# One place per half chunk instead of two for the output projection's matmuls in an RWKV-7 recurrence

## The chip, the cores and the metric

The kernel runs on one core of one Trainium2 chip. The metric is the device time of one execution in microseconds. Three runs of the kernel before gave 1660.01, 1664.27 and 1664.91 us, the median is 1664.27 us. One further execution was profiled; the rows below come from it.

## The reference, cut to what matters

One residual layer with an RWKV-7 mixer on 2048 tokens of width 1024, 16 heads of 64, in float32. The part around the change is the recurrence over tokens, the group norm of its output, the gate and the output projection:

```python
def step(S, inp):
    r_t, w_t, k_t, v_t, kk_t, a_t = inp
    sa = jnp.einsum('bhvk,bhk->bhv', S, -kk_t)
    S = (S * w_t[:, :, None, :]
         + sa[..., None] * (kk_t * a_t)[:, :, None, :]
         + v_t[..., None] * k_t[:, :, None, :])
    y_t = jnp.einsum('bhvk,bhk->bhv', S, r_t)
    return S, y_t
...
y = (y - mean) * lax.rsqrt(var + RW_GN_EPS)
y = y * gn_w.astype(f32).reshape(H, N) + gn_b.astype(f32).reshape(H, N)
y = y + jnp.sum(r_h * k_h * r_k.astype(f32), axis=-1, keepdims=True) * v_h
y = y.reshape(Bsz, T, W).astype(h.dtype) * g
return y @ w_out, v_first
...
x = x + y.astype(x.dtype)
```

## The kernel before

The tokens are cut into 64 chunks of 32. Earlier phases compute the projections and, for each chunk, small matrices that turn the recurrence within a chunk into matrix products; they go through memory and come back chunk by chunk (`load_c`, `load_v`, two and three chunks ahead). Chunks 0 to 8 run interleaved with the preparation of the last block of tokens. Chunks 9 to 63 run in the last phase, which is the one that the change touches. Its order on TensorE, VectorE, ScalarE and GpSimd is the order in which the program issues the instructions, and each engine works its queue in that order.

A chunk is done in two halves of 8 heads each (w = 0 and 1). Each half issues four small groups of 8 matmuls. A matmul of these groups is listed as two instructions in the trace, so a group is x16 there and x8 in the order:

- S, `r_state` (L249): the chunk's matrices times the state `x`, into `ybank`. Two ScalarE copies (L254) bring a part of it to `misc`.
- D, `r_d` (L274): the state's update, into `dp`. Two VectorE instructions (L51, x<-dp,misc) scale it into the next chunk's `x`. The D that stands behind S of one half belongs to the other half: behind S of w = 0 comes D of the chunk before, w = 1.
- Y, `r_y` (L289): the rest of the output, added to `ybank` of the other half. ScalarE copies it to `y` (L297).
- U, `r_u` (L261): a triangular product of `misc` into `ubank`. ScalarE copies it to `x` (L265), where the D and Y of the next half need it.

So U of a half waits for ScalarE's copies of S of the same half, D and Y wait for the copies of U of the half before, and S waits for VectorE's scaling of the D of the half before.

Every four chunks make a tile of 128 tokens, and `tail` turns it into background work: squares on ScalarE, sums on VectorE, a reciprocal root by Newton steps on GpSimd (L383, L384), normalisation and gating on VectorE, transposes on TensorE (L424), and in the end 48 projection matmuls (L460, 512 columns each: 2 output halves, 8 input blocks, 3 products of high and low parts), which go into the queue `dense`. `background` takes items of `work` for about 1.6 us of estimated time at each call, evacuations of finished output halves (L48) first. `fill(n)` takes n matmuls from `dense`, times 0.7, 1 or 1.3 by the queue's length, and keeps the rest as credit. Both are called by `chunk` through `state()`, which stands behind each S, and through `fill(i)`, which is the function `after` here: i = 0 behind D and i = 1 behind U in the first half, i = 2 and 3 in the second. After chunk 63 the program empties what is left.

`F` and `BG` are set as (2, 4) and 1.6.

Of the kernel before, what the change touches and what calls it, by code (L numbers as in the profile page):

```python
# [28 lines left out]
F, BG, EV, EV0, GWE, BNE, LOW, SLOW, FAST, INV, INVC = (2, 4), 1.6, (0, 0, 0), (0, 0, 0), 0, 0, 36, 0.7, 1.3, (8, 10), 0.5  # L29
# [10 lines left out]
def rwkv7_kernel(ctx, tc, a, T):  # L40
# [226 lines left out]
    def r_d(ch, w):  # L267
        if ch + 1 == NCH:
            return
        d, x = dk[ch % len(dk)], xs[ch % len(xs)]  # L270
        dp = bank[3]
        for p in range(4):
            for h in range(2):
                nc.tensor.matmul(dp[half(1 - h), p], d[:, h, 4 * w + p], x[:, h, 4 * w + p], start=True, stop=True,  # L274
                                 tile_position=(0, 64 * (1 - h)))
        g, c = divmod(ch, NC)
        with urgent():
            for h in range(2):

                H = half(1 - h)  # L280
                tt(xs[(ch + 1) % len(xs)][H, h, 4 * w : 4 * w + 4], dp[H],
                   pls[g][H, c, 4 * w : 4 * w + 4, None].broadcast_to([64, 4, N]), mul)

    def r_y(ch, w):
        st, x, c = stat[ch % len(stat)], xs[ch % len(xs)], ch % 4
        for p in range(4):
            for h in range(2):
                rb = bu(h)
                nc.tensor.matmul(bank[w][rb, ch % 2, p], st[rb, h, 4 * w + p, cr], x[rb, h, 4 * w + p], start=False,  # L289
                                 stop=(p == 3), skip_group_check=True, tile_position=(rb.start, rb.start))  # L290
        t = ch // 4
        if c == 0 and w == 0:
            new_y(t)
        with urgent():
            for h in range(2):
                o = 64 * h + L * (c % 2)
                ev(2, h)(ys[t][o : o + L, c // 2, 4 * w : 4 * w + 4], bank[w][bu(h), ch % 2])  # L297

    def chunk(ch, state, fill):

        g, c = divmod(ch, NC)
        if c == 2 and g + 1 < NB:
            load_g(g + 1)
        r_state(ch, 0)
        state()
        if ch != first[0]:
            r_d(ch - 1, 1)
        fill(0)
        if ch != first[0]:
            r_y(ch - 1, 1)  # L310
        if ch + 2 < NCH:
            load_v(ch + 2)
        if ch + 3 < NCH:
            load_c(ch + 3)
        r_u(ch, 0)
        fill(1)
        r_state(ch, 1)
        state()
        r_d(ch, 0)
        fill(2)  # L320
        r_y(ch, 0)
        r_u(ch, 1)
        fill(3)
# [4 lines left out]
    def fill(n):  # L328

        served[0] = min(served[0], 6) + n * (FAST if len(dense) > 2 * LOW else 1 if len(dense) > LOW else SLOW)  # L330
        while served[0] > 0 and dense:
            dense.popleft()[0]()
            served[0] -= 1
# [152 lines left out]
    def inversion(g, z, tmp):  # L486

        def load():
            for h in range(2):
                nc.sync.dma_start(z[half(h)], sm_d[g][bu(h), h, :, :, ca].rearrange("s c p t -> (c p) s t"))  # L490

        def step(j):
            n = L - 1 - j
            t3 = tmp()[:, 0 : j * n].rearrange("p (s t) -> p s t", t=n)
            tt(t3, z[:, 0:j, j : j + 1].broadcast_to([P, j, n]), z[:, j : j + 1, j + 1 :].broadcast_to([P, j, n]), mul)
            tt(z[:, 0:j, j + 1 :], z[:, 0:j, j + 1 :], t3, add)
            if j == 1:
                nc.vector.memset(z.rearrange("p s t -> p (s t)")[:, 0 : L * L : L + 1], 1.0)
                for h in range(2):
                    nc.sync.dma_start(sm_d[g][bu(h), h, :, :, ca].rearrange("s c p t -> (c p) s t"), z[half(h)])  # L500

        return [load] + [lambda j=j: step(j) for j in range(L - 2, 0, -1)]

    with ExitStack() as p0:
# [150 lines left out]
        with ExitStack() as pb:  # L655
            def pool(n, bufs, **k):
                return pb.enter_context(tc.tile_pool(name=n, bufs=bufs, reuse_waits="tile", **k))
# [380 lines left out]
            with tc.manual_schedule(engines=MANUAL):  # L1038
# [92 lines left out]
                def wo_split(p, q):  # L1131
                    hi, lo = (wo_t[x][p][:, 512 * q : 512 * q + 512] for x in range(2))
                    split(hi, lo, lo.bitcast(F32))
# [39 lines left out]
    with ExitStack() as p1:  # L1173
        def pool(n, bufs, **k):
            return p1.enter_context(tc.tile_pool(name=n, bufs=bufs, reuse_waits="tile", **k))

        c1, yp = pool("c1", 1), pool("yp", 1)
        sps, tps = pool("sps", 1, space=PSUM), pool("tps", 1, space=PSUM)
        for w in range(2):
            bank[w] = sps.tile([P, 2, 4, N], F32, name=f"ybank{w}")  # L1180
        bank[2] = sps.tile([P, 4, N], F32, name="ubank")
        bank[3] = sps.tile([P, 4, N], F32, name="dp")
        work = deque()
        evs[:] = EV
        al.update(rs=nc.gpsimd, newton=0, wait=2)
        al["sml"] = lambda nm: yp.tile([P, 2, NP], F32, name=nm, tag="sml", bufs=8)
        al["sq"] = lambda nm: yp.tile([P, 4, N], F32, name=nm, tag="big", bufs=4)
        al["v"] = lambda nm: yp.tile([P, NP, N], F32, name=nm, tag="v", bufs=4)
        al["o"] = lambda nm: yp.tile([P, NCT, P], F32R, name=nm, tag=nm[:2], bufs=2)
        al["yt"] = lambda nm: tps.tile([P, 4, P], F32, name=nm, tag="tps")  # L1190
        al["gt"] = lambda nm: yp.tile([P, NCT, 64], F32, name=nm, tag="gt", bufs=2)

        def background(us):

            served[1] = min(served[1] + us, us)
            fresh = True
            while evacs or work:
                u, fn = (evacs or work)[0]
                if not fresh and (u is None or u > served[1]):
                    break  # L1200
                (evacs or work).popleft()
                if u is None:
                    continue
                fresh = False
                fn()
                served[1] -= u

        def more_y(t):
            while t > 5 and t - 3 not in turned:
                background(1)  # L1210
            return yp.tile([P, 2, NP, N], F32, name=f"y{t}", tag="y", bufs=3)

        more[0], first[0] = more_y, NC + 1

        with tc.manual_schedule(engines=MANUAL):
            work.extend((0.7, lambda q=q: wo_split(NP - 1, q)) for q in range(2))
            for x in tail(1):
                work.extend(x)
            z = c1.tile([P, L, L], F32, name="z_")
            tm = c1.tile([P, 4 * N], F32, name="tm_")  # L1220
            inv = deque()
            for g in (NB - 2, NB - 1):
                load, *cols = inversion(g, z, lambda: tm)
                inv.extend([(0, load)] + [(None, None), (0, lambda: None)] * 4)
                inv.extend((INVC, x) for x in cols)
            inv_g = inv[L + 6][1]

            inv_last = inv[-1][1]

            def after(i):  # L1230
                if i % 2:
                    background(BG)
                fill(F[i % 2])

            for ch in range(NC + 1, NCH):
                chunk(ch, lambda: background(BG), after)
                if ch % 4 == 0 and ch > NC:
                    for x in tail(ch // 4 - 1):
                        work.extend(x)
                    for i in range(INV[1] if ch >= INV[0] else 0):  # L1240
                        if inv:
                            work.append(inv.popleft())
                if ch == NCH - 2 * NC - 4:
                    assert len(inv) <= L - 1 and not any(x[1] is inv_g for x in work)
                if ch == NCH - NC - 4:
                    assert not inv and not any(x[1] is inv_last for x in work)
            r_d(NCH - 1, 1)
            r_y(NCH - 1, 1)
            for x in tail(NCH // 4 - 1):
                work.extend(x)  # L1250
            while work or dense or evacs:
                background(2)
                fill(6)
# [52 lines left out]
```

## Time and profile before

| | |
|---|---|
| median of three runs | 1664.27 us |
| the profiled execution | 1656.89 us, of which the span is 1655.0 us |
| busy, share of the span | PE 93%, PEld 79%, DVE 72%, ACT 50%, POOL 22% |
| mean granted clock of TensorE | 0.981 |
| L460, three forms, 256 matmuls each | 110.5, 111.2 and 107.9 us busy, mean 421 to 434 ns |
| L249 weight loads, 1760 | 65.3 us busy, mean 139 ns |
| ScalarE copies L297, L254, 220 each | 80.1 and 79.7 us busy, mean 364 and 362 ns |
| VectorE L51, x<-dp,misc, 216 | 91.2 us busy, mean 422 ns |

PE is TensorE's matmuls, PEld its weight loads, DVE VectorE, ACT ScalarE, POOL GpSimd, SP the queue that issues most transfers. Matmuls overlap in the pipeline, so the distance from the start of one to the start of the next says more than the length of one. In square brackets a row gives the idle time of the engine in front of an instruction and what ended it. A clock of 1.00 is 2.4 GHz, 0.50 is 1.2 GHz.

### The profile page before, as it was taken

The page shows a single profiled execution, that of the slowest core. Times are in us where ns is not written, and L with a number is a line of the kernel's source. Part 1 is how long each engine was busy: PE and PEld are TensorE (multiplying, and loading weights), DVE is VectorE, ACT ScalarE, POOL GpSimd, SP SyncE. Part 2 cuts the span into 40 slices and gives each one's busy share as a digit, 9 for nine tenths or more (in the row PEclk, how much of TensorE's full clock was granted, in tenths as well). Part 3 has the DMA queues.
Part 4 walks back from the last instruction along what each step waited for, and adds up shares of the span by engine and source line. Part 5 has one row for each costly group of instructions (what it writes and reads, how often), then busy time and mean ns, then how long its engine had stood idle before and what let it go on. Part 6 is the DMA issues. An engine that isn't in the chain of part 4 may idle for free.

```text
span 1655.0 us, 45952 instructions
## 1 busy us (share of the span) xinstructions
PE 1543.2 (93%) x17776; PEld 1309.1 (79%) x17776; DVE 1191.5 (72%) x2844; ACT 834.5 (50%) x2126; POOL 359.3 (22%) x727
## 2 busy tenths in 40 slices
PE   3699999999999999999999999888999999999998
PEld 2589889998888888988898888677777777777776
DVE  7976776667655579787888878568566767776564
ACT  5653332223356455454545454577556666555551
POOL 4500000000002232232323233212322222322321
PEclk9999999999999999999999999799999999999999
DMA  5773433334574565557676777688866686677642
GB/s 182 223 255 125 144 116 113 126 128 150 146 229 114 131 139 154 123 151 148 155 153 168 166 155 179 178 224 226 198 173 171 171 193 189 161 185 182 173 120 87
DMA packets 445739, 269.14 MB, mean 163 GB/s; under 512 B 302768, under 2 KB 386096, under 8 KB 445520
## 3 DMA queue, kind: packets, MB, share of 16 engines
q1 hardware_dynamic: 444176, 261.67, 58.9%
q10 hardware_dynamic: 1344, 4.52, 1.0%
q8 instruction: 141, 2.31, 0.6%
q14 instruction: 78, 0.64, 0.1%
HBM read 158.74 MB, written 111.54 MB: 163 GB/s over the span
## 4 chain that ended last, share of the span: by engine, by line
PE 59%; DVE 17%; DMA 6%; ACT 6%; issue 4%; SPq 2%; POOL 1%; DVEq 0%; ACTq 0%; POOLq 0%
PE ops L460 9%; PE gps L540 9%; PE kps L540 8%; PE rps L846 8%; PE vps L540 4%; PE ybank L249 3%; PE ybank L289 3%; PE dp L274 3%; PE mps L882 2%; PE ubank L261 2%; DMA xn<-x 1%; DMA xa<-xT 1%; PE lps L602 1%; DVE x L51 1%; PE tps L867 1%
## 5 line engine op out<-in xcount | busy, mean ns | idle before, releaser
L540 PE MATMUL gps<-mixbh,wgh 128*128 128x256 f32 x512 | 146.1, 285 | 4.7 <-ACT vo L635 4.7
L540 PE MATMUL gps<-mixbh,wgl 128*128 128x256 f32 x512 | 145.7, 285 | 0.0
L540 PE MATMUL gps<-mixbl,wgh 128*128 128x256 f32 x512 | 145.7, 285 | 0.0
L540 PE MATMUL kps<-mixbl,wkh 128*128 128x256 f32 x448 | 128.7, 287 | 14.7 <-DVE mixbl L186 14.7
L222 POOL MEMSET x<- 32x512 f32 x128 | 66.3, 518 | 328.6 <-PE ybank L289 254.1
L846 PE MATMUL rps<-mixah,wrh 128*128 128x256 f32 x448 | 133.1, 297 | 2.1 <-ACT sq L60 2.1
L540 PE MATMUL kps<-mixbh,wkh 128*128 128x256 f32 x448 | 132.6, 296 | 0.6 <-DVE u L48 0.6
L51 DVE TENSOR_TENSOR x<-dp,misc 64x256 f32<-64x256 f32 x216 | 91.2, 422 | 55.5 <-PE dp L274 49.8
L540 PE MATMUL kps<-mixbh,wkl 128*128 128x256 f32 x448 | 127.9, 285 | 0.0
L846 PE MATMUL rps<-mixal,wrh 128*128 128x256 f32 x448 | 127.5, 285 | 0.0
L846 PE MATMUL rps<-mixah,wrl 128*128 128x256 f32 x448 | 127.4, 284 | 0.0
L297 ACT COPY y<-ybank 32x256 f32<-32x256 f32 x220 | 80.1, 364 | 93.3 <-PE ybank L289 91.5
L254 ACT COPY misc<-ybank 32x256 f32<-32x256 f32 x220 | 79.7, 362 | 89.4 <-PE ybank L249 86.1
L460 PE MATMUL ops<-woh,oh 128*128 128x512 f32 x256 | 110.5, 432 | 1.6 <-ACT oh L439 1.6
L60 ACT ACTIVATE th<-wa,dprm 128x256 f32<-128x256 f32 x64 | 30.4, 476 | 160.8 <-PE wa L798 99.5
L460 PE MATMUL ops<-woh,ol 128*128 128x512 f32 x256 | 111.2, 434 | 0.0
L249 PEld LDWEIGHTS ybank<-x,stat 128*64 128x64 f32 x1760 | 65.3, 139 | 57.9 <-issue 26.8
L540 PE MATMUL vps<-wvh,mixah 128*128 128x512 f32 x256 | 104.6, 409 | 6.5 <-ACT mixah L96 5.1
L460 PE MATMUL ops<-wol,oh 128*128 128x512 f32 x256 | 107.9, 421 | 0.0
L540 PEld LDWEIGHTS gps<-mixbh,wgh 128*128 128x128 f32 x512 | 99.0, 193 | 5.2 <-ACT vo L635 5.1
L540 PE MATMUL vps<-wvl,mixah 128*128 128x512 f32 x256 | 102.1, 399 | 0.0
L540 PEld LDWEIGHTS kps<-mixbl,wkh 128*128 128x128 f32 x448 | 87.0, 194 | 16.0 <-DVE mixbl L186 16.0
(325 smaller groups left out, 4583.1 us busy)
## 6 DMA issues: line engine op xcount, KB each, us to landing
stat<-sm_d SPq DMA_DIRECT2D x64, 512.0 KB, 4.7
dk<-bt_d SPq DMA_DIRECT2D x128, 128.0 KB, 4.4
sm_d<-ra SPq DMA_DIRECT2D x112, 128.0 KB, 3.3
sm_d<-mo SPq DMA_DIRECT2D x112, 128.0 KB, 2.7
bt_d<-bo SPq DMA_DIRECT2D x56, 256.0 KB, 3.2
up<-up_d SPq DMA_DIRECT2D x66, 128.0 KB, 2.6
xn<-x SPq DMA_DIRECT2D x32, 256.0 KB, 4.9
mkr_d<-mok SPq DMA_DIRECT2D x64, 128.0 KB, 1.9
```

The source lines that it names most:

```text
L51: return nc.vector.tensor_tensor(out=out, in0=in0, in1=in1, op=op)
L222: nc.gpsimd.memset(x[bu(h), h], 0.0)
L249: nc.tensor.matmul(y[half(h), p], st[:, h, 4 * w + p], x[:, h, 4 * w + p], start=(p == 0), stop=(p == 3), tile_position=(0, 64 * h))
L254: nc.scalar.copy(gs[bu(h)], y[kv(h)])
L261: nc.tensor.matmul(bank[2][rb, p], st[rb, h, 4 * w + p, ca], gs[rb, p], start=True, stop=True, tile_position=(rb.start, rb.start))
L274: nc.tensor.matmul(dp[half(1 - h), p], d[:, h, 4 * w + p], x[:, h, 4 * w + p], start=True, stop=True, tile_position=(0, 64 * (1 - h)))
L289: nc.tensor.matmul(bank[w][rb, ch % 2, p], st[rb, h, 4 * w + p, cr], x[rb, h, 4 * w + p], start=False, stop=(p == 3), skip_group_check=Tru ...
L297: ev(2, h)(ys[t][o : o + L, c // 2, 4 * w : 4 * w + 4], bank[w][bu(h), ch % 2])
L460: nc.tensor.matmul(ps, l[:, ct], r(ct, ns), start=(ct == 0 and k == 0), stop=(ct == NCT - 1 and k == 2))
L540: nc.tensor.matmul(ps, x, y, start=first, stop=last)
L846: nc.tensor.matmul(ps, x, y, start=first, stop=last)
L882: nc.tensor.matmul(ps[H, c], bk[H, c], ra[H, c], start=True, stop=True, tile_position=(64 * h, 64 * h))
```

## The change

`after` is called at the same four places of a chunk, but issues projection matmuls only at the two odd ones, and asks there for `sum(F)` = 6 instead of 4. The call of `background` in it was under the same condition before.

```diff
--- before.py
+++ after.py
@@ -1228,9 +1228,10 @@
             inv_last = inv[-1][1]
 
             def after(i):
+
                 if i % 2:
                     background(BG)
-                fill(F[i % 2])
+                    fill(sum(F))
 
             for ch in range(NC + 1, NCH):
                 chunk(ch, lambda: background(BG), after)
```

On TensorE, in a regular half chunk from S (L249) on, one piece of the difference in the order (the number behind a name is the buffer, + is the changed kernel):

```order
 L249 MATMUL ybank_15631<-x_13803,stat_13795 64x64 x8
 L274 MATMUL dp<-x_13805,dk_13802 64x64 x8
+L289 MATMUL ybank_15632<-x_13805,stat_13798 32x64 x8
+L261 MATMUL ubank<-misc,stat_13795 32x64 x8
 L460 MATMUL ops_15942<-woh_14372,ol_15547 128x512
 L460 MATMUL ops_15942<-woh_14561,oh_15546 128x512
-L289 MATMUL ybank_15632<-x_13805,stat_13798 32x64 x8
-L261 MATMUL ubank<-misc,stat_13795 32x64 x8
 L460 MATMUL ops_15942<-wol_14562,oh_15546 128x512
 L460 MATMUL ops_15942<-woh_14561,ol_15547 128x512
```

Y (L289) and U (L261) now stand directly behind D (L274), and the two projection matmuls that stood in front of them join the run behind U.

On VectorE, around the scaling of D (L51, x<-dp,misc), where an output half's evacuation (L48) falls to another background call; one piece of the difference:

```order
-L51 TENSOR_TENSOR x_13805<-dp,misc 64x256 x2
+L51 TENSOR_TENSOR x_13805<-dp,misc 64x256 x2
+L51 TENSOR_TENSOR y_13808<-y_13808,rst_16117 128x256
+L410 TENSOR_TENSOR y_13808<-y_13808,aux 128x256
 L48 SCALAR_TENSOR_TENSOR xr_15943<-ops_15942,xr_15943 128x256
 L48 SCALAR_TENSOR_TENSOR xr_15945<-ops_15942,xr_15945 128x256
-L51 TENSOR_TENSOR y_13808<-y_13808,rst_16117 128x256
-L410 TENSOR_TENSOR y_13808<-y_13808,aux 128x256
-L51 TENSOR_TENSOR x_13805<-dp,misc 64x256 x2
 L414 TENSOR_TENSOR y_13808<-y_13808,v_0_16118 128x256
+L51 TENSOR_TENSOR x_13805<-dp,misc 64x256 x2
```

The two L48 stand behind two steps of the normalisation now, and one of those steps' successors (L414) has come in front of the next scaling.

## Rows read from the trace of the kernel before

**Rows 1.** stretches: us, busy us of PE, PEld, DVE, ACT, POOL; clock; DMA

```profile
1150.00:1618.00 468.00, 452.14 (x7746) 338.52 (x7744) 315.33 (x732) 277.63 (x746) 126.78 (x316) 0.98 0.67 174
```

**Rows 2.** timeline of TensorE, one half chunk (start us, us, instruction)

```profile
1409.80 0.69 PE L249 MATMUL ybank<-x,stat 128*64 128x64 f32 x16
1410.31 0.64 PE L274 MATMUL dp<-x,dk 128*64 128x64 f32 x16
1410.88 0.50 PE L460 MATMUL ops<-woh,oh 128*128 128x512 f32 x1
1411.54 0.64 PE L289 MATMUL ybank<-x,stat 32*32 32x64 f32 x16
1412.01 0.61 PE L261 MATMUL ubank<-misc,stat 32*32 32x64 f32 x16
1412.55 0.50 PE L460 MATMUL ops<-woh,ol 128*128 128x512 f32 x1
...
1412.89 0.40 PE L460 MATMUL ops<-woh,oh 128*128 128x512 f32 x1
1413.12 0.40 PE L460 MATMUL ops<-wol,oh 128*128 128x512 f32 x1
...
1413.68 0.69 PE L249 MATMUL ybank<-x,stat 128*64 128x64 f32 x16
1414.20 0.29 PE L274 MATMUL dp<-x,dk 128*64 128x64 f32 x4
```

**Rows 3.** timeline of ScalarE and TensorE, L289 directly behind L274

```profile
1147.64 0.75 ACT L265 COPY x<-ud 32x256 f32<-32x256 f32 x2
...
1148.45 0.68 PE L274 MATMUL ud<-x,dk 128*64 128x64 f32 x16 [0.80 <-ACT x L265]
...
1149.06 0.64 PE L289 MATMUL yb<-x,stat 32*32 32x64 f32 x16
```

**Rows 4.** timeline of ScalarE in the half chunk of rows 2

```profile
1410.58 0.75 ACT L254 COPY misc<-ybank 32x256 f32<-32x256 f32 x2 [0.72 <-PE ybank L249]
...
1413.01 0.75 ACT L265 COPY x<-ubank 32x256 f32<-32x256 f32 x2
```

**Rows 5.** waits from 1150 to 1618 (us in total, times, longest)

```profile
ACT misc L254 <- PE ybank L249: 86.1, 95, 3.1
DVE x L51 <- PE dp L274: 49.8, 40, 3.0
...
DVE y L51 <- POOL rst L383: 26.7, 11, 3.3
...
PE ybank L249 <- DVE x L51: 6.8, 8, 1.6
```

**Rows 6.** timeline of ScalarE, squares in front of a state copy

```profile
1225.10 1.34 ACT L60 ACTIVATE sq<-y 128x256 f32<-128x256 f32 x4
1226.46 0.75 ACT L254 COPY misc<-ybank 32x256 f32<-32x256 f32 x2
```

**Rows 7.** timeline of VectorE in the half chunk of rows 2

```profile
1411.98 0.87 DVE L51 TENSOR_TENSOR x<-dp,misc 64x256 f32<-64x256 f32 x2
```

**Rows 8.** timeline of VectorE and TensorE, a stop of the state group

```profile
1500.32 0.17 DVE L57 TENSOR_SCALAR g<-var 128x16 int32<-128x16 int32 x1
...
1504.66 1.25 DVE L51 TENSOR_TENSOR y<-y,rst 128x256 f32<-128x256 f32 x1 [3.26 <-POOL rst L383]
...
1507.12 0.88 DVE L51 TENSOR_TENSOR x<-dp,misc 64x256 f32<-64x256 f32 x2
1507.69 0.98 PE L249 MATMUL ybank<-x,stat 128*64 128x64 f32 x15 [1.54 <-DVE x L51]
```

**Rows 9.** busy time and granted clock in three stretches

```profile
1126.20:1131.80 5.60, 5.54 (x125) 4.44 (x124) 4.06 (x11) 4.66 (x12) 0.00 (x0) 1.00 0.38 112
1232.00:1240.00 8.00, 6.38 (x107) 4.70 (x107) 7.60 (x17) 3.53 (x11) 2.61 (x4) 1.00 0.63 184
1510.00:1516.00 6.00, 6.00 (x56) 4.56 (x56) 2.82 (x7) 2.18 (x6) 0.00 (x0) 0.50 0.60 174
```

## The prediction

> **What bounds the kernel now.** I read the table of stretches first, then the timeline of one regular half chunk, then the waits. The change touches the stretch from about 1150 us to 1618 us, where the recurrence runs chunks 9 to 63 (55 chunks, 110 halves). In it TensorE is busy for 452 of 468 us and VectorE for 315 [rows 1]. The 37 us from there to the end of the span are almost pure projection, which does not change. So TensorE's queue sets the pace, and the question is what its own order costs it.
>
> A regular half is 3.88 us long, from the start of one state group (L249, called S here) at 1409.80 to the next at 1413.68 [rows 2]. In it stand S, then L274 (D), two projection matmuls (L460), L289 (Y), L261 (U), four projection matmuls. Start to start: S to D 0.51, D to the run of two 0.57, that run 0.66, Y to U 0.47, U to the run of four 0.54, that run 1.13 us. TensorE waits for nobody here, yet the runs have a fixed part. Inside a run matmuls follow each other in 0.23 us (1412.89 to 1413.12), so two should take 0.46 and take 0.66, four should take 0.93 and take 1.13: 0.20 us for entering and leaving a run, whatever its length.
>
> **What the change does, part by part.** It takes away the run behind D and puts its matmuls into the run behind U. The number of matmuls stays; the order has 225 runs of them before and 115 after, so 110 runs go, one per half. The title's "background work" does not move: the two calls behind the S groups and the two behind U are where they were, and ScalarE and VectorE get the same instructions, a few of them swapped.
>
> TensorE's issue time, per half: before, D to Y is 0.57 + 0.66 = 1.23 us, of which 2 x 0.23 = 0.46 are matmuls that are only moved. 0.77 us are left for D and its seams. After, Y stands directly behind D. The trace has that neighbourhood once, in the part before: D at 1148.45, Y at 1149.06, 0.61 us [rows 3]. That would give back 0.77 - 0.61 = 0.16 us. Its bounds: S to D, also two small groups, takes 0.51 us, which would give 0.26 us; a seam as dear as before, 0.77 us, would give nothing. I take 0.61, the row that shows the thing itself. The run of six should then take 0.20 + 6 x 0.23 = 1.58 us, and the half 0.51 + 0.61 + 0.47 + 0.54 + 1.58 = 3.71 us (0.16 under 3.88 but for rounding). 110 halves x 0.16 us = 17.6 us.
>
> The cover that goes. U needs the two ScalarE copies of S (L254). They begin 0.78 us behind S and end at 1411.33, 1.53 us behind it [rows 4]. Before, U starts at 2.21 us, so 0.68 us of slack, of which the run of two was 0.66. After, U can start at 0.51 + 0.61 + 0.47 = 1.59 us. A copy that ended at 1148.39 let TensorE start at 1148.45 [rows 3], so the copies are seen about 0.06 us late, at 1.59 us. The wait is just about nothing, and it can't grow into a loss from a faster seam: with D to Y in 0.51 us, U would come 0.10 us too early and wait those 0.10 us, so the gain stays at about 0.16 us, and at most 0.20 us if only U's second matmul needs the second copy. Behind U, if it waits, stands the run of six, which nobody on the chain of the recurrence needs.
>
> Where ScalarE is late, U now waits in full. Of 110 pairs of these copies 95 waited for TensorE [rows 5], so about 15 were late. The worst I see is four squares of 1.34 us in front of a copy that began at 1226.46 [rows 6], 0.68 us late. The other 95 pairs had 86.1 us to spare, 0.9 us each, so lateness is rare and short: I take 2 us for all of them, bounds 0 and 15 x 0.68 = 10 us.
>
> D's own needs get easier: its ScalarE copies (L265) end at 1413.76, 0.44 us ahead of the D at 1414.20 that needs them [rows 2, 4]. After, Y and U and these copies come about 0.6 us earlier in the half and the next D only 0.16 us earlier, so the slack is about 0.9 us.
>
> VectorE. The next S needs D's result, which VectorE scales (L51, 0.87 us, done at 1412.85) [rows 7]; there are 0.83 us left before S at 1413.68, after the change about 0.67. In regular halves nothing waits. But VectorE's queue is in order, and once per tile of four chunks it stops in front of the normalisation until GpSimd has its reciprocal root: 26.7 us in 11 stops. S waits for VectorE 8 times, 6.8 us in all [rows 5]. One such place: VectorE gives the seed at 1500.32, stops until 1504.66, does two slow steps, then D's scaling at 1507.12, and S starts at 1507.69 after 1.54 us [rows 8]. Those 7.4 us, two halves, are set by GpSimd and VectorE and not by TensorE, so the gain of these halves is lost: 8 x 2 x 0.16 = 2.6 us, at all 14 tiles 4.5 us. I take 3 us. Where a 512-column half of the output ends in the moved run, its evacuation (two instructions of VectorE, 0.8 us) now comes one background call later, in front of D's scaling, inside the slack: nothing, at the worst 1 us in all. Loads of the residual are issued with the first matmul of such a half and are needed 24 matmuls later; SP's queue, moved by under 2 us, has room.
>
> Sum: -17.6 + 2 + 3 + 0.5 = -12 us. The profiled execution took 1656.9 us (span 1655.0) and would take 1645; the median of the runs shown is 1664.27, 7.4 us above the profiled one, and with the same 12 us taken off it comes to 1652.
>
> **Rivals.**
> (a) *The second engine becomes the bound.* If VectorE and GpSimd held not two but six of the eight halves of each tile, 14 x 6 = 84 of 110 gains would be lost and 26 x 0.16 = 4 us be left: 1660. For it: the stops above, and VectorE's 315 of 468 us [rows 1]. Against: VectorE itself waited for D 49.8 us in 40 places [rows 5], so it is mostly ahead.
> (b) *The clock falls, and the kernel gets slower.* Place: behind the stops of S. There TensorE now does S, D, Y and U, 2.1 us of small tiles, before its first wide run, where before the run of two came after 1.1 us. After the stop at 1507 the granted clock was 0.50 (1.2 GHz) for the 6 us from 1510, so each fall costs about 3 us of TensorE's work; at the stop before 1234 it stayed at 1.00 (2.4 GHz) in spite of TensorE being idle for 1.6 us of 8 [rows 9]. It decides from four more falls (12 us against 12); with one more at ten of the 14 tiles it is 30 - 12 = +18 us: 1682. Against it: from 1126.2 to 1131.8 TensorE ran only small groups (L289, L261, L867, L796, L798, L710, L249, L274, L882, L289), and the clock held 1.00 [rows 9].
> (c) *The seam is not saved.* If the 0.20 us is the small groups' own tail and D to Y costs 0.77 us in this stretch, the change is worth nothing: 1664, or a few us more with the late copies. Only the one row of 0.61 us speaks against it, and its D had just waited. The Trainium skill (TensorE: Matmul & The Clock Gate, "Step-by-step: what each phase is for") leans to this side: TensorE pulls weight loads ahead of running matmuls, so that the next tile's weights load while this one computes. By that a run of two would cost no more per matmul than a run of six, and the sum would be 0. The rows with 0.20 us for each run disagree, as far as this trace goes.
>
> **How the numbers follow.** Forecast 0.70, within 1644 to 1657 (gains from 20 down to 7); (a) 0.12 at 1657 to 1662; (c) 0.08; (b) 0.10, from 1664 up. A measurement here can tell about 0.3%, 5 us, from no change. Faster by more than that: the forecast and half of (a), 0.76. Same: the other half of (a), (c) and a little of (b), 0.15. Slower: 0.09. The range for 8 in 10 reaches from 1642, the gain of 0.20 us in all halves, to 1661, inside (a).
>
> **What would show it.** Right: one run of L460 per half, of 1.58 us; D to Y near 0.6 us; S to S near 3.71 us in regular halves; TensorE's waits for L254 small and in few places; waits for VectorE's L51 up by some 3 us from 6.8. Wrong: S to S at 3.8 us or more with U waiting for L254 in every half (copies later than I think), D to Y at 0.77 us (c), a longer list of stretches at 0.50 (b), or waits for L51 of 15 us and more (a).

## The result, and the profile after

The changed kernel takes 1641.44 us (median of 4 runs, 1639.68 to 1646.22), the kernel before 1662.14 us over its 4 runs (1653.57 to 1664.91). The ratio on record is 0.9895, 95% interval 0.986 to 0.9931: 17 us less, between 11 and 23 (the two medians, of four runs each, are 20.7 us apart). The profiled execution of the changed kernel took 1642.18 us with a span of 1640.4 us, 14.7 us less than the profiled one of before. A repetition on another occasion gave a ratio of 0.9904 (0.9872 to 0.9936), with medians 14.0 us apart.

The stretch of chunks 9 to 63, as in [rows 1] (columns as there):

```profile
1150.00:1604.00 454.00, 437.21 (x7795) 351.94 (x7791) 316.18 (x733) 279.03 (x750) 126.68 (x316) 0.98 0.68 180
```

Nearly the same work of TensorE is done in 454 us instead of 468. The length of the stretch is read more exactly from the first start of S and the last start of Y (the two times behind each count; the three numbers before are the shortest, median and longest of one, in ns). First the kernel before, then the changed one:

```profile
L249 PE MATMUL ybank<-x,stat x1760: 221/222/370, 1150.4 to 1614.7; 128*64 128x64 f32 x196
L289 PE MATMUL ybank<-x,stat x1760: 213/214/312, 1158.4 to 1618.5; 32*32 32x64 f32 x196
```

```profile
L249 PE MATMUL ybank<-x,stat x1760: 222/222/369, 1151.5 to 1599.4; 128*64 128x64 f32 x196
L289 PE MATMUL ybank<-x,stat x1760: 214/214/311, 1159.4 to 1602.8; 32*32 32x64 f32 x196
```

From 1150.4 to 1618.5 it was 468.1 us, from 1151.5 to 1602.8 it is 451.3: 16.8 us less. The rest of the difference of the spans lies outside: the stretch began 1.1 us later, and what is behind it (from there to the last projection matmul's start) took 33.4 instead of 32.3 us.

A regular half on TensorE, the answer to [rows 2]:

```profile
1398.68 0.69 PE L249 MATMUL ybank<-x,stat 128*64 128x64 f32 x16
1399.19 0.64 PE L274 MATMUL dp<-x,dk 128*64 128x64 f32 x16
1399.76 0.64 PE L289 MATMUL ybank<-x,stat 32*32 32x64 f32 x16
1400.23 0.66 PE L261 MATMUL ubank<-misc,stat 32*32 32x64 f32 x16
1400.83 0.50 PE L460 MATMUL ops<-woh,ol 128*128 128x512 f32 x1
...
1401.16 0.39 PE L460 MATMUL ops<-woh,oh 128*128 128x512 f32 x1
1401.39 0.40 PE L460 MATMUL ops<-wol,oh 128*128 128x512 f32 x1
...
1402.42 0.69 PE L249 MATMUL ybank<-x,stat 128*64 128x64 f32 x16
```

S to S is 3.74 us, where it was 3.88. D to Y is 0.57 us, Y to U 0.47, U to the run 0.60, the run of six 1.59 us, which is 0.20 + 6 x 0.23. U starts at 1400.23, and the copies it needs end at 1400.22 (ScalarE, the answer to [rows 4]):

```profile
1399.47 0.75 ACT L254 COPY misc<-ybank 32x256 f32<-32x256 f32 x2 [1.24 <-PE ybank L249]
...
1401.23 0.76 ACT L265 COPY x<-ubank 32x256 f32<-32x256 f32 x2
```

U's second matmul waits for the second of them, so U takes 0.05 us longer (0.66 where it was 0.61). The two ends meet almost exactly. In the fifteen halves where four transposes stand between S and D, U starts some 0.7 us later behind S, and U to the run is 0.54 us as before the change: the 0.05 us are that wait.

Where a run's fixed 0.20 us lie is seen in the weight loads (PEld) of the half of [rows 2], in the kernel before:

```profile
1410.25 0.55 PEld L274 LDWEIGHTS dp<-x,dk 128*64 128x64 f32 x16
1410.88 0.19 PEld L460 LDWEIGHTS ops<-woh,oh 128*128 128x128 f32 x1
1410.98 0.19 PEld L460 LDWEIGHTS ops<-wol,oh 128*128 128x128 f32 x1
1411.54 0.47 PEld L289 LDWEIGHTS ybank<-x,stat 32*32 32x32 f32 x16 [0.37 <-issue]
1411.96 0.50 PEld L261 LDWEIGHTS ubank<-misc,stat 32*32 32x32 f32 x16
```

The figure in front of the shape, `128*64`, `128*128` or `32*32`, is the rows and columns of TensorE that a matmul uses, here called its tile. From S to D and from Y to U the tile stays the same, and the next group's first load starts 0.05 to 0.06 us ahead of its first matmul (1410.25 against 1410.31, 1411.96 against 1412.01). Where the tile changes, load and matmul start together (1410.88, 1411.54), and the step from the last matmul to the next group's first is about 0.10 us longer. Behind the first matmul of a run the second comes after 0.33 instead of 0.23 us. D to Y is a change of the tile with or without a run in between; a run there adds one change more and the late second matmul, 0.10 us each. The median steps are the same in the regular halves of the kernels below, but no kernel changed the tile alone, so that the tile is the reason is read from the rows and not shown by an experiment.

The waits, the answer to [rows 5]:

```profile
ACT misc L254 <- PE ybank L249: 124.6, 97, 3.8
DVE x L51 <- PE dp L274: 57.2, 46, 4.7
...
ACT y L297 <- PE ybank L289: 35.3, 85, 2.2
...
DVE y L51 <- POOL rst L383: 23.1, 10, 3.1
...
PE ybank L249 <- DVE x L51: 7.9, 6, 2.0
...
PEld ubank L261 <- ACT misc L254: 2.6, 3, 2.1
```

S waits for VectorE 7.9 us in all, 1.1 us more than before. U waits for the copies 2.6 us (0.4 before), 2.1 of them in one place at the beginning. ScalarE waits for S 124.6 us instead of 86.1, but for Y 35.3 us, where the kernel before has:

```profile
ACT y L297 <- PE ybank L289: 90.7, 96, 2.8
```

So its waits have moved from Y to S, and their sum is 17 us smaller: ScalarE does the same work, 278 and 279 us, in 468 and in 454 us. A stop of S of the kind of [rows 8] is still there; on VectorE and then on TensorE:

```profile
1582.62 1.25 DVE L51 TENSOR_TENSOR y<-y,rst 128x256 f32<-128x256 f32 x1 [2.67 <-POOL rst L383]
...
1586.87 0.88 DVE L51 TENSOR_TENSOR x<-dp,misc 64x256 f32<-64x256 f32 x2
```

```profile
1587.44 1.04 PE L249 MATMUL ybank<-x,stat 128*64 128x64 f32 x15 [2.04 <-DVE x L51]
```

VectorE had stopped for GpSimd, did two slow steps and four others, and S came 2.04 us late. Behind it the clock fell, as in [rows 9] (the last columns are the granted clock, the share of the DMA engines and GB/s):

```profile
1590.00:1594.00 4.00, 4.00 (x32) 2.87 (x26) 1.65 (x5) 1.45 (x4) 0.00 (x0) 0.50 0.43 133
```

In windows of 5 us the stretch has three falls of the clock in both kernels: before at 1155, 1170 and 1510, after at 1155, 1170 and 1590. By the trace's clock records the time at 1.2 GHz in it is 17.1 us before and 13.7 us after. At 1.2 GHz wide matmuls follow each other in 0.43 us instead of 0.23, so where TensorE is busy about half of such time is lost, and up to 1.7 of the 16.8 us are the clock.

### The profile page after: what moved, and what is told of

The parts are those of the page before. It is cut to its first block, busy times and chain, and to the rows that moved or that the text cites. A ratio compares the mean times of both kernels' runs of the same rounds, so it can differ in the third digit from the quotient of the medians.

```text
span 1640.4 us, 45953 instructions
## 1 busy us (share of the span) xinstructions
PE 1529.5 (93%) x17776; PEld 1325.5 (81%) x17776; DVE 1192.3 (73%) x2844; ACT 835.3 (51%) x2126; POOL 359.8 (22%) x727
## 5 line engine op out<-in xcount | busy, mean ns | idle before, releaser
L254 ACT COPY misc<-ybank 32x256 f32<-32x256 f32 x220 | 79.6, 362 | 127.8 <-PE ybank L249 124.6
L540 PE MATMUL kps<-mixbl,wkh 128*128 128x256 f32 x448 | 130.4, 291 | 14.7 <-DVE mixbl L186 14.7
L51 DVE TENSOR_TENSOR x<-dp,misc 64x256 f32<-64x256 f32 x216 | 91.2, 422 | 62.7 <-PE dp L274 57.2
L222 POOL MEMSET x<- 32x512 f32 x128 | 66.4, 519 | 300.2 <-PE ybank L289 228.3
L249 PEld LDWEIGHTS ybank<-x,stat 128*64 128x64 f32 x1760 | 64.7, 138 | 57.1 <-issue 33.5
L460 PE MATMUL ops<-woh,oh 128*128 128x512 f32 x256 | 107.2, 419 | 0.0
L460 PE MATMUL ops<-woh,ol 128*128 128x512 f32 x256 | 105.4, 412 | 0.0
L460 PE MATMUL ops<-wol,oh 128*128 128x512 f32 x256 | 104.0, 406 | 0.0
L540 PEld LDWEIGHTS gps<-mixbl,wgh 128*128 128x128 f32 x512 | 99.9, 195 | 0.0
```

The source lines that it names most:

```text
L51: return nc.vector.tensor_tensor(out=out, in0=in0, in1=in1, op=op)
L222: nc.gpsimd.memset(x[bu(h), h], 0.0)
L249: nc.tensor.matmul(y[half(h), p], st[:, h, 4 * w + p], x[:, h, 4 * w + p], start=(p == 0), stop=(p == 3), tile_position=(0, 64 * h))
L254: nc.scalar.copy(gs[bu(h)], y[kv(h)])
L460: nc.tensor.matmul(ps, l[:, ct], r(ct, ns), start=(ct == 0 and k == 0), stop=(ct == NCT - 1 and k == 2))
L540: nc.tensor.matmul(ps, x, y, start=first, stop=last)
```

## The experiments

Theory S (for seams) is that of the prediction: the gain is the fixed cost of a run of wide matmuls between small groups, paid once per run wherever it stands. Its rivals were that the recurrence's own chain had become shorter, that only the seam behind D was dear, and that stops and falls of the clock had become fewer. Ratios are to the kernel before, from runs on the same chip; the run behind D and the run once per chunk have two executions each, the others four to twelve. Length and rest are taken from each trace as above: from the first S to the last Y, and from there to the last projection matmul's start. Length, rest and granted clock (its mean over the length) are of one execution each.

| kernel | runs of L460 | ratio (95%) | length, us | clock | rest, us |
|---|---|---|---|---|---|
| before | 225 | 1 | 468.1 | 0.98 | 32.3 |
| changed | 115 | 0.9895 (0.986 to 0.9931) | 451.3 | 0.98 | 33.4 |
| changed, repeated | 115 | 0.9904 (0.9872 to 0.9936) | 450.7 | 0.99 | 34.0 |
| first half only | 170 | 0.9953 (0.9936 to 0.9971) | 458.2 | 0.98 | 33.1 |
| run between Y and U | 225 | 1.0048 (1.0029 to 1.0068) | 475.5 | 0.98 | 32.5 |
| run behind D | 115 | 1.0235 (1.02 to 1.0269) | 505.8 | 0.99 | 35.5 |
| once per chunk | 58 | 1.0108 (1.0069 to 1.0146) | 487.5 | 0.95 | 32.9 |
| background at two places | 115 | 1.0104 (1.0067 to 1.0141) | 458.1 | 0.96 | 58.5 |
| four spacers | 115 | 0.9949 (0.9927 to 0.9972) | 439.0 | 0.98 | 54.8 |
| transposes behind U | 117 | 0.9957 (0.9934 to 0.998) | 451.3 | 0.98 | 41.8 |

**The change in the first half of a chunk only.**

```diff
                 if i % 2:
                     background(BG)
-                    fill(sum(F))
+                if i > 1:
+                    fill(F[i % 2])
+                elif i:
+                    fill(sum(F))
```

> The change made in the first half of each chunk only: run of six behind U there, two and four as before in the second half (170 runs of projection matmuls instead of 225 before and 115 after the change). Theory S (seams: each run costs 0.15 to 0.20 us for leaving and re-entering the small groups, wherever it stands): half of the gain, 55 x 0.15 = 8 us, ratio to before 0.995, and side by side in one trace regular halves of 3.74 us with one run and 3.88 us with two. Rival C (chain: the gain comes from the recurrence's own chain, whose copies come earlier, so what waits less is the state): the half that is left as before keeps the chain long, little gain, 0 to 3 us, ratio 0.998 to 1.000. Rival K (the gain is fewer stops and falls of the clock): regular halves alike in both, 3.8 us.

Half of the runs removed gave 0.9953, 8 us. TensorE shows both kinds of half side by side:

```profile
1363.30 0.69 PE L249 MATMUL ybank<-x,stat 128*64 128x64 f32 x16
1363.81 0.64 PE L274 MATMUL dp<-x,dk 128*64 128x64 f32 x16
1364.38 0.64 PE L289 MATMUL ybank<-x,stat 32*32 32x64 f32 x16
...
1365.44 0.50 PE L460 MATMUL ops<-woh,oh 128*128 128x512 f32 x1
...
1367.03 0.69 PE L249 MATMUL ybank<-x,stat 128*64 128x64 f32 x16
1367.54 0.64 PE L274 MATMUL dp<-x,dk 128*64 128x64 f32 x16
1368.11 0.50 PE L460 MATMUL ops<-woh,oh 128*128 128x512 f32 x1
...
1368.77 0.64 PE L289 MATMUL ybank<-x,stat 32*32 32x64 f32 x16
...
1369.78 0.50 PE L460 MATMUL ops<-woh,ol 128*128 128x512 f32 x1
...
1370.90 0.28 PE L249 MATMUL ybank<-x,stat 128*64 128x64 f32 x2
```

From 1363.30 to 1367.03, with one run, 3.73 us; from 1367.03 to 1370.90, with two, 3.87 us. TensorE waits for nobody in either. So the gain is in the regular half and goes with the run that is gone; a chain or fewer stops would not show in two neighbours. The stretch became 9.9 us shorter, more than half of the full 16.8. If each of the 110 halves is set against the same half in the trace of before, the 55 changed ones have a median of 0.15 us less (5.8 us in sum), the 55 others a median of 0.00 us (but 4.1 us less in sum). The second sum lies in ten irregular halves, with stops, falls of the clock or another number of projection matmuls; it is not the price of a run.

**The run of two between Y and U.**

```diff
-        fill(2)
         r_y(ch, 0)
+        fill(2)
         r_u(ch, 1)
```

(what the edit amounts to in chunks 9 to 63, and the same for `fill(0)`; on the kernel before.)

> As before the change with two runs per half, but the run of two stands between Y and U instead of between D and Y. Theory S: as many seams as before, no gain; by the rows D to Y 0.57, Y to the run 0.54, the run 0.66 against D to the run 0.57, the run 0.66, Y to U 0.47, so 0.06 us more per half, up to 7 us slower than before, ratio 1.000 to 1.004. Rival D (only the seam at D, between 128-row and 32-row groups, was dear, and Y directly behind D is what gained): D to Y stands in this kernel too, so most of the gain is kept, 10 us or more faster than before, ratio 0.994 or less.

8 us slower than before (1.0048), just beyond the upper end of what theory S expected. The half:

```profile
1362.47 0.69 PE L249 MATMUL ybank<-x,stat 128*64 128x64 f32 x16
1362.98 0.64 PE L274 MATMUL dp<-x,dk 128*64 128x64 f32 x16
1363.55 0.64 PE L289 MATMUL ybank<-x,stat 32*32 32x64 f32 x16
1364.12 0.50 PE L466 MATMUL ops<-woh,oh 128*128 128x512 f32 x1
...
1364.78 0.64 PE L261 MATMUL ubank<-misc,stat 32*32 32x64 f32 x16
1365.35 0.50 PE L466 MATMUL ops<-woh,ol 128*128 128x512 f32 x1
...
1366.48 0.69 PE L249 MATMUL ybank<-x,stat 128*64 128x64 f32 x16
```

D to Y is 0.57 us here as in the changed kernel, but the run has its seams at another place: Y to the run 0.57, the run of two 0.66, U to the run 0.57, and S to S 4.01 us. So Y directly behind D is not what gains, the run that is gone is. But a run does not cost the same wherever it stands. Between Y and U the run of two costs 0.57 + 0.66 - 0.47 - 0.46 = 0.30 us, between D and Y it cost 0.20: Y and U have the same tile, so here the run brings two changes of the tile instead of one. A regular half is 0.13 us longer than before; in 110 halves that would be 14 us, where the stretch became 7.4 us longer. TensorE's idle time in front of S is 3.8 us shorter here (10.5 against 14.3); the remaining 3 us are not accounted for.

**The run of six behind D.**

```diff
                 if i % 2:
                     background(BG)
+                else:
                     fill(sum(F))
```

> One run of six per half, but behind D and not behind U. Theory S with the chain of copies: the seams go as in the change, but U's copies (two of Y, then two of U on ScalarE, done 1.8 us behind U's start) are now uncovered, since the next D comes 0.57 + 0.51 = 1.08 us behind U: D waits about 0.7 us in every half, 110 x (0.7 - 0.15) = 60 us slower than before, ratio 1.036, S to S about 4.4 us. If only seams counted: 16 us faster than before, S to S 3.74 us.

1.0235, 39 us slower, with the same number of runs as the changed kernel. The cover is what is missing, but the wait stands at another place than I expected. TensorE first, then ScalarE:

```profile
1366.05 0.61 PE L261 MATMUL ubank<-misc,stat 32*32 32x64 f32 x16
1367.08 0.69 PE L249 MATMUL ybank<-x,stat 128*64 128x64 f32 x16 [0.42 <-ACT y L297]
```

```profile
1366.28 0.74 ACT L297 COPY y<-ybank 32x256 f32<-32x256 f32 x2 [2.12 <-PE ybank L289]
1367.05 0.75 ACT L265 COPY x<-ubank 32x256 f32<-32x256 f32 x2
```

U to S takes 1.03 us instead of some 0.57: S starts at 1367.08, 0.06 us behind the end of Y's copies (L297, 1367.02). I had D wait for U's copies; S is held first, by Y's. The trace names L297 as what ended TensorE's wait at S in 43 places. Why S needs those copies, which read other columns of the same bank, was not tried. D then takes longer too, 0.73 us to the run in a regular half where it was 0.57, and S to S is 4.49 us, near the 4.4 expected. The price came out at 39 instead of 60 us, because other halves lose less: against the same half of before, the median half is 0.40 us longer, a regular one 0.61.

**One run per chunk.**

```diff
                 if i % 2:
                     background(BG)
-                    fill(sum(F))
+                if i == 3:
+                    fill(2 * sum(F))
```

> One run of twelve per chunk, behind the U of the second half (58 runs in all). Seams alone: another 55 x 0.15 = 8 us off the changed kernel, ratio to before 0.985. With the chain: in the half without a run the next D comes 1.08 us behind U, while U's copies take 1.8 us, and the next S comes 1.6 us behind D while D's scaling takes 1.6 us on an idle VectorE and more on a busy one: a wait of 0.7 to 1.5 us per chunk, 40 to 80 us, so 20 to 60 us slower than before, ratio 1.01 to 1.04.

1.0108, 18 us slower, just under the expected 20 to 60. In the half without a run the same wait is seen (TensorE, then ScalarE):

```profile
1336.62 0.66 PE L261 MATMUL ubank<-misc,stat 32*32 32x64 f32 x16
1337.64 0.69 PE L249 MATMUL ybank<-x,stat 128*64 128x64 f32 x16 [0.37 <-ACT y L297]
```

```profile
1336.85 0.74 ACT L297 COPY y<-ybank 32x256 f32<-32x256 f32 x2 [0.26 <-PE ybank L289]
```

Y's copies end at 1337.59, S starts at 1337.64, 1.02 us behind U. The two regular halves of a chunk take 2.58 + 5.35 = 7.93 us at full clock, where the changed kernel takes 2 x 3.74: some 25 us more in 55 chunks. The profiled execution lost time in a second way. Its granted clock fell in seven places of the stretch, 47.8 us at 1.2 GHz against 17.1 before and 13.7 in the changed kernel, so up to 17 of the 36 us by which its stretch is longer than the changed kernel's are the clock. The other execution had an overall clock like that of before (0.977) and was still 13 us slower than before. Fewer runs are only better as long as a run is left in each half to cover ScalarE.

**The background work at two places as well.**

```diff
-                    background(BG)
+                    background(2 * BG)
                     fill(sum(F))
...
-                chunk(ch, lambda: background(BG), after)
+                chunk(ch, lambda: None, after)
```

> The changed kernel with the background work, too, at two places per chunk (behind U, with a budget of 3.2 us) and none behind S. Theory S: the transposes that stood between S and D (16 groups; S to transposes 0.61, transposes to D 0.59 against S to D 0.51 us) now stand in front of a run, where they cost 0.27 us less: 4 us off the changed kernel, ratio to before 0.987. Rival (cover): all of ScalarE's squares and casts now stand between U's copies and the next S's copies, U waits for L254 in more places, and items that end a call come half as often, so more projection is left for the end: 5 to 15 us slower than the changed kernel, ratio 0.993 to 0.999.

1.0104: 33 us behind the changed kernel, more than either expected. The seams of 16 transposes are small against two other things. The rest behind the last chunk takes 58.5 instead of 34 us, because an item that ends a call now comes half as often; 11 of these 24.5 us are only 47 projection matmuls (175 against 128) that are moved there. And the stretch became 7.4 us longer without these 47 matmuls. There the background work is so late that the kernel runs it at once when a new tile of `y` is due (`new_y` in `r_y`), and in nine places transposes stand between Y and U, in six of them two groups, the second waiting for VectorE:

```profile
1334.14 0.63 PE L424 MATMUL yt<-consts,y 128*128 128x128 f32 x4 [1.61 <-DVE gt L51]
```

TensorE's waits for VectorE at the transposes come to 22.4 us in the stretch, and the repeated changed kernel has none there. The clock fell in six places, 34.1 us at 1.2 GHz against 10.2, which is up to 12 us.

**Four spacers in front of the normalisation.**

```diff
-        al.update(rs=nc.gpsimd, newton=0, wait=2)
+        al.update(rs=nc.gpsimd, newton=0, wait=4)
```

> The changed kernel with four spacers instead of two between the Newton steps on GpSimd and the normalisation on VectorE. If the prediction's loss term is right (VectorE's stops in front of the normalisation hold back S and take back the gain of those halves, 3 us, and lead to falls of the clock): VectorE's waits for GpSimd fall from 23 us to under 8, S's waits for VectorE from 9 us to under 4, 4 to 8 us faster than the changed kernel, ratio to before 0.985 to 0.987. Rival: the stops only use slack that is there, the waits of S move to other places: within 2 us of the changed kernel.

The waits went as the first theory had it, and the time the other way: 0.9949, some 7 us slower than the changed kernel. Its waits, to the end of the span:

```profile
PE ybank L249 <- DVE x L51: 3.8, 5, 1.8
...
DVE y L51 <- POOL rst L383: 0.4, 1, 0.4
```

VectorE waits for GpSimd 0.4 us where the repeated changed kernel has 28.0, and S for VectorE 3.8 us where that has 8.0. But 48 more matmuls are left for the end (176 against 128), 11 us of the longer rest of 54.8 us. The other 10 us are mostly waits of TensorE for VectorE and ScalarE there, which the recurrence used to cover (7.4 us against 1.9), and a lower clock (10.2 us at 1.2 GHz against 3.4). With those 48 matmuls in it the stretch would be 450 us, as long as with the stops. But in this execution it has four falls of the clock against two, 20.5 us at 1.2 GHz against 10.2; at the same clock it would be some 5 us shorter, an estimate from one execution of each kernel. So what the stops themselves cost is not settled by this run.

**The transposes kept out of the calls behind S.**

```diff
+                if not turn and fn in turns:
+                    break
...
-                chunk(ch, lambda: background(BG), after)
+                chunk(ch, lambda: background(BG, False), after)
```

(`turns` holds the transposes of `tail`.)

> The changed kernel, with the transposes of the background work (L424) kept out of the calls behind S, so that they stand in front of the run behind U (24 groups there and none behind S, in place of 10 and 16). Theory S: a transpose group between S and D costs 0.61 + 0.59 - 0.51 = 0.69 us, one between U and the run 0.60 + 0.41 - 0.59 = 0.42 us, so 16 x 0.27 = 4 us off the changed kernel, ratio to before 0.986 to 0.988. Rival T (tail): work that waits for the next call is left for the end, where VectorE's and GpSimd's steps are not covered; one more tile's transposes stand behind the last chunk: 3 to 8 us given back there, ratio 0.989 to 0.993.

0.9957, slower than the changed kernel by some 9 us, and beyond the rival's range. The rest is 8 us longer, and the stretch, with 25 matmuls fewer in it, is no shorter:

```profile
PE ybank L249 <- DVE x L51: 10.7, 8, 1.9
PEld ybank L249 <- POOL x L222: 5.4, 5, 1.8
```

S waits 10.7 us for VectorE and 5.4 us for GpSimd's clearing of `x` (L222), which was 0.7 us in the changed kernel. Over the stretch TensorE's waits sum to 23.3 us against 16.7, and the clock costs up to 3.4 us more (17.1 us at 1.2 GHz against 10.2). That is about as much as 25 matmuls fewer (6 us) and the 4 us of the transposes' seams would save, so the 4 us could not be seen in the total; whether they are there is open. No version here beats the changed kernel.

## Why the prediction was right, point by point

- *The time:* the gain is inside the range, 3 to 22 us below 1664; the figure in microseconds is not a hit. 1641.44 us lies just under the range's lower end of 1642, because 1664.27, from which it was counted, was a high median for that kernel: with a fourth run it is 1662.14, on other occasions 1656.7 to 1657.7. The profiled execution, 1645 predicted, took 1642.2.
- *The fixed 0.20 us of a run:* right for this place. The run of six takes 1.59 us (1.58 predicted), and halving the number of removed runs about halved the gain. "For entering and leaving a run, whatever its length" holds for the length, not for the place: between Y and U a run costs 0.30 us.
- *D to Y:* 0.57 us, between the bounds of 0.51 and 0.61, not at the 0.61 that I took from the one row before the stretch, where D had waited and took 0.68 us itself [rows 3] instead of 0.64. S to S 3.74 us against 3.71 predicted: D to Y gave 0.04 us more, and U takes 0.05 us longer for its second copy, a meeting that the sum had at nothing. That the two nearly cancel is not luck alone: the prediction argued that a faster D to Y would only make U wait.
- *The cover of U:* right. U starts 1.55 us behind S and its copies end at 1.54. The gain of a regular half, put at 0.16 to 0.20 us, came out just under that, at 0.14 to 0.15 us.
- *ScalarE's slack for D:* right. U's copies end at 1401.99 (L265), 0.94 us ahead of the next D, 0.51 us behind the S at 1402.42; some 0.9 us were predicted, 0.44 it was before.
- *The losses, 5.5 us:* too large, and the reason why -12 us was predicted where the profiled executions differ by 14.7 and the ratio says 17. The waits of S for VectorE rose by 1.1 us, not 3, those of U by 2.2 us. The stretch became 16.8 us shorter, of which up to 1.7 are the clock; that leaves 15.1 us, 0.137 us for each of 110 halves. Half against half, the median gain is 0.149 us, 16.4 us in all, so about 1 us is missing by the lengths and 3 us by the waits. The step that is mis-sized is "8 x 2 x 0.16" for halves set by GpSimd and VectorE, and no row shows the 0.5 us that the sum has besides. The attempt to show the stops' price by spacing them out gave no clean answer.
- *Rival (a)*, VectorE as the bound, did not come: it waits for D 57.2 us now, 49.8 before. *Rival (b)*, the clock, neither: three falls in both. Its price was seen in single places all the same, and in full where a half has no run or the background work stalls TensorE (once per chunk, background at two places). *Rival (c)*, the seam that is not saved, is refuted by the D to Y of 0.57 us and by the first-half kernel, and with it the reading by which weights that load under running matmuls make short runs as cheap as long ones. The weight rows show both: inside a run the next weights do load under the running matmul (1410.98 for the matmul at 1411.21), at a change of the tile load and matmul start together.

## What to carry to other kernels

Where wide filler matmuls are sprinkled between small groups, look at start-to-start distances at the seams: a fixed cost per run is seen there although TensorE is "busy" all the time and waits for nobody. Put the filler into as few runs as the chain allows, where two neighbours differ in their tile anyway, and let each run stand where it covers the longest wait that comes next; a run at the wrong place (behind D) or one too few cost more than all the seams gave. Look at the granted clock before a difference is put down to waits. Work that is postponed to get a better order reappears behind the loop, where nothing covers it, or is forced at a worse place inside it.

## What the runs showed that I had not expected

- S is held by ScalarE's copies of the Y before it: 1.02 to 1.03 us from U to S in the two kernels without a run there.
- ScalarE's end is seen by TensorE within 0.05 to 0.06 us, and a copy that ends 0.01 us before its reader starts costs that reader 0.05 us.
- A stop of S of 2.0 us (1.5 in [rows 8]) was followed by several us at 1.2 GHz; another as long, of 1.56 us before the S at 1234.46 in [rows 9], was not, so a stop's price varies by about 3 us from one to the next.
